# Thirty-two experts in thirteen rounds instead of sixteen, sorted by token count, with weights read in 8 KB runs

## The chip, the cores and the metric

One core of a Trainium2 chip runs the whole program. The metric is the device time of one execution in microseconds, as the median of several runs. A profiled execution gives the trace, and its own time stands beside it.

## What is computed

One layer over 512 tokens of 1,024 features, in float32. First a token mixer (a gated MLP and a differential attention, summed and projected), then a hierarchical mixture of experts, each with a residual and a layer norm. The change is in the second part:

```python
def _hier_moe(x, w_group, b_group, w_expert, b_expert, w_gate, w_up, w_down):
    g_sel = jnp.argmax(g_logits, axis=-1)                 # one of 4 groups
    top_v, top_i = lax.top_k(e_logits, EXPERT_TOPK)       # 2 of its 8 experts
    top_w = jax.nn.softmax(top_v, axis=-1) * g_w
    ...
    def expert_block(args):
        tok, wgt, e = args
        xb = t[tok]
        hb = jax.nn.silu(xb @ w_gate[e]) * (xb @ w_up[e])  # 1024 -> 512
        return (hb @ w_down[e]) * wgt[:, None]             # 512 -> 1024
```

So 1,024 pairs of a token and an expert spread over 32 experts, 32 on average. Each expert has 2 MB of gate weights, 2 MB of up weights and 2 MB of down weights, 201 MB in all, and every byte is read once. For the inputs that are run, the reference's routing gives experts 0 to 5 at most 42 tokens, the largest expert 49, and of the 26 others the twelve smallest have 21 to 30.

## The kernel before

The first half of the program is the token mixer. From about 470 us on the experts run, in **rounds** of two (`NP = E // 2` = 16 rounds, experts 2p and 2p+1 in round p). A round has 128 slots, 64 for each of the two experts (`CAP`). Per round, TensorE does this in program order (function `pair`):

- `slot_info` (L1157): which token sits in which slot, and with what weight;
- `gather_mm` (L1150), in four parts: the next round's token rows are gathered by one-hot matmuls, 64 of 128 columns, from the two fp16 parts `hs` of the hidden state;
- `glu_transpose` (L1179), `down` (L1190, two halves of 512 output columns) and `combine` (L1207), which adds the round's output to `y`;
- `gate_up` (L1103) of the next round: gate and up, each over 8 steps k of 128 input features.

In `gate_up` and `down` the two experts of a round lie side by side: 64 slots are the stationary operand, so each expert's matmul uses 64 of the array's 128 columns and writes its own half of the output's partitions (`po[j * 64:(j + 1) * 64]`); the moving operand is 512 columns of weights. Each such float32 matmul is two instructions in the trace.

**Weights.** They are cut into 192 **chunks** of 1 MB, 12 to a round (0 to 3 gate, 4 to 7 up, 8 to 11 down). A chunk holds, for both experts of a round, two steps k, and is fetched by two DMAs of 512 KB on SP's queue in `chunk_load` (L694), each with runs of 2 KB (512 floats). The last round's last two chunks are read as 512-byte runs (L690). The chunks go round a ring of 21 buffers (`AHEAD`, `ring_at`): the load of chunk i + 21 follows in SP's program behind the point where TensorE has used chunk i, and SP waits in order for the buffer to come free. One buffer of the ring (`raw`, named `craw`) is lent in round 0 to `load_lgb`, the rows of a scale and an offset that DVE uses in `scale_h`; SP's load into it waits for that, and what stands behind it on SP waits too.

**Overflow.** An expert with more than 64 tokens would be finished by a loop behind a branch (`overflow`, L1213 to L1222). All engines read the largest count into a register and branch; for these inputs the loop doesn't run. The branch stands behind round 12 (`OVERFLOW_AFTER`); the counts are made in round 1 (`counts`).

The order on every engine is the program's own here (`manual_schedule`). The last two rounds are interleaved by hand in `last_pairs`, and `finish` is the closing layer norm.

Of the kernel before, what the change touches and what calls it, by code (L numbers as in the profile page):

```python
# [21 lines left out]
D = 1024  # L22
NT = 4
# [8 lines left out]
OVERFLOW_AFTER = 12  # L32
# [11 lines left out]
def hybrid_block(ctx: ExitStack, tc: tile.TileContext, x, w_in, b_in, sg_ln_g, sg_ln_b, sg_w, sg_b,  # L44
# [30 lines left out]
    RS = const.tile([128, NT, E], F32, name="RS")  # L75
    O1 = const.tile([128, NT, E], F32, name="O1")
    Wm = const.tile([128, NT, E], F32, name="Wm")
# [596 lines left out]
    NP = E // 2  # L674
    order = [(p, c) for p in range(NP - 2) for c in range(12)]
# [3 lines left out]

    def chunk_load(dst, i, kk):  # L680
        p, c = order[i]
        if c < 8:
            src = dram((w_gate, w_up)[c // 4], (2 * p * D + 256 * (c % 4) + 128 * kk) * FF,
                       [[FF, 128], [D * FF, 2], [1, FF]])
        elif p < NP - 1 or c < 10:
            src = dram(w_down, (2 * p * FF + 256 * (c % 2) + 128 * kk) * D + 512 * ((c - 8) // 2),
                       [[D, 128], [FF * D, 2], [1, 512]])
        else:
            for j in range(2):
                nc.sync.dma_start(dst[:, j].rearrange("p (k c) -> p k c", k=4),  # L690
                                  dram(w_down, (2 * p + j) * FF * D + 512 + 256 * (c - 10) + 128 * kk,
                                       [[D, 128], [128 * D, 4], [1, 128]]))
            return
        nc.sync.dma_start(dst, src)  # L694

    held = {}

    def halves(tag):
        if tag not in held:
            if tag == "raw":  # L700
                held[tag] = [big.tile([128, 2, 512], F32, name="craw", tag="raw", bufs=2) for _ in range(2)]
            elif tag == "F1":
                held[tag] = [slot(tag, F32, (128, 2, 512))]
            else:
                c = slot(tag, F32, (128, 2, 2, 512))
                held[tag] = [c[:, kk] for kk in range(2)]
# [72 lines left out]
    aux = const.tile([128, NT, E // 2, 8], F16, name="aux")  # L779
    for t in range(NT):  # L780
        G.memset(aux[:, t, :, 1], float(128 * t))
    G.iota(aux[:, :, :, 0], pattern=[[0, NT], [0, E // 2]], base=1, channel_multiplier=1,
           allow_small_or_imprecise_dtypes=True)
# [16 lines left out]
    gbc = const.tile([128, 3, 8], F32, name="gbc")  # L800

    def fold_router():
        pgb = bank("w")
        P.transpose(pgb[:, :16], gbr, ident[:16, :16])
        V.tensor_copy(gbc[:, 0], pgb[:, 0:8])
        V.tensor_scalar(gbc[:, 1], gbc[:, 0], 1.0 / HSCALE, None, op0=OP.mult)
        V.tensor_copy(gbc[:, 2], pgb[:, 8:16])
        V.tensor_tensor(wr[:, :, 36:72], wr[:, :, 0:36], gbc[:, 2, :, None].to_broadcast([128, 8, 36]), op=OP.mult)
# [157 lines left out]
    def evacuate(pg, first=False):  # L966
# [3 lines left out]
        for d in (3,4,0,5,1,6,2,7) if first else range(8):  # L970
            src = pg[d // 4][:, (d % 4) * 128:(d % 4 + 1) * 128]
            g, b = gbc[:, 0 if first else 1, d:d + 1], gbc[:, 2, d:d + 1]
# [18 lines left out]
    def gate_weights():  # L991
# [10 lines left out]
        flat = lambda v: v.rearrange("p t e -> p (t e)")  # L1002
        ax = aux.rearrange("p t q j -> p (t q) j")[:, :, 2:8].rearrange("p q (e j) -> p q e j", j=3)
        wv, rv = [flat(v).rearrange("p (q e) -> p q e", e=2) for v in (Wm, wb)]
        V.tensor_scalar(ax[:, :, :, 0], wv, WSCALE, None, op0=OP.mult)
        V.scalar_tensor_tensor(rv, wv, WSCALE, ax[:, :, :, 0], op0=OP.mult, op1=OP.subtract)
        V.tensor_copy(ax[:, :, :, 1], rv)
        V.tensor_sub(ax[:, :, :, 2], rv, ax[:, :, :, 1])
# [85 lines left out]
    def gate_up(p, xe, filler=None):  # L1094
        pg, pu = bank("acc"), bank("acc")
        for o, base in ((pg, 0), (pu, 4)):

            ks = range(8) if p or base else (3,4,5,0,1,6,2,7)
            for k in ks:
                if filler and base and k % 2:  # L1100
# [449 lines left out]
```

## Time and profile before

| | us |
|---|---|
| median of 3 runs | 975.62 (975.32 to 977.42) |
| the profiled execution | 977.95 |
| its span, first to last instruction | 976.4 |
| TensorE busy in the span | 953.7 (98%) |
| DMA queue of SP (q1): bytes, share of 16 engines | 252.37 MB, 73.9% |
| mean granted TensorE clock | 0.993 of full speed |

All times are in us from the start of the span. A matmul's end is modelled, so a TensorE that is "busy" may still be waiting on its pipe; the starts are what to go by, and the distance from one start to the next. The share of the DMA engines counts a packet from its start to its end, and packets overlap a little, so it can pass 1.00.

### The profile page before, as it was taken

How to read it: one execution, taken by the hardware profiler on the slowest of the kernel's cores; microseconds unless marked ns; L12 is line 12 of the kernel's file. 1: busy time of each engine (PE TensorE's matmuls, PEld its weight loads, DVE VectorE, ACT ScalarE, POOL GpSimd, SP SyncE). 2: the span in 40 equal slices, each digit the busy share in tenths (PEclk: the TensorE clock that was granted, in tenths of full speed). 3: DMA queues.
4: the chain of work that ended last, by engine and by line, in shares of the span. 5: the costliest groups of instructions: out<-in, count | busy, mean ns of one | idle time of the engine just before them, and what ended most of it. 6: DMA issues, size and time to landing. Idle time of an engine off the chain costs nothing. (4 is left out here: it accounts for less than half of the span.)

```text
span 976.4 us, 14138 instructions
## 1 busy us (share of the span) xinstructions
PE 953.7 (98%) x5427; PEld 615.7 (63%) x5428; DVE 451.0 (46%) x940; ACT 300.3 (31%) x550; POOL 56.1 (6%) x97
## 2 busy tenths in 40 slices
PE   8999999999999999999999999999999999979996
PEld 6989898886888888888544444444444444434434
DVE  4567676767943423545764322333223333223236
ACT  3456565666641332323411101111101111011213
POOL 5010010110010200200000000000000000000002
PEclk9999999999999999999999999999999999989999
DMA  8634445343233758765899999999999999999972
GB/s 217 171 94 135 120 119 135 97 131 87 66 96 88 262 190 282 250 225 202 308 341 377 386 386 386 387 386 386 386 387 386 386 387 386 386 386 386 386 234 87
DMA packets 147993, 256.14 MB, mean 262 GB/s; under 512 B 11481, under 2 KB 33041, under 8 KB 147921
## 3 DMA queue, kind: packets, MB, share of 16 engines
q1 hardware_dynamic: 146672, 252.37, 73.9%
q0 software_dynamic: 1248, 2.82, 1.4%
q8 instruction: 45, 0.74, 0.3%
q14 instruction: 28, 0.22, 0.1%
HBM read 244.66 MB, written 2.10 MB: 253 GB/s over the span
## 5 line engine op out<-in xcount | busy, mean ns | idle before, releaser
L113 DVE TENSOR_TENSOR sW<-wraw,sW 128x1024 fp32r<-128x1024 f32 (+1 forms) x38 | 46.5, 1225 | 97.3 <-ACT sW L112 97.2
L112 ACT CAST sW<-wraw 128x1024 fp32r<-128x1024 f32 (+1 forms) x38 | 39.1, 1030 | 116.2 <-PE ps_w L138 65.8
L1210 DVE TENSOR_TENSOR h<-h,ps_w 128x512 f32<-128x512 f32 x112 | 69.3, 680 | 10.2 <-PE ps_w L1207 10.2
L136 PE MATMUL ps_acc<-sX,sW 128*128 128x512 f32 x184 | 73.4, 399 | 0.0
L138 PE MATMUL ps_acc<-sX,sW 128*128 128x512 f32 x184 | 72.2, 392 | 0.0
L137 PE MATMUL ps_acc<-sX,sW 128*128 128x512 f32 x184 | 72.0, 392 | 0.0
L1160 DVE TENSOR_REDUCE tid<-ps_w 128x1 f32<-128x2 f32 x14 | 2.2, 159 | 150.5 <-PE ps_w L1157 150.5
L1200 DVE SCALAR_TENSOR_TENSOR olo<-ps_acc,ws,ohi 128x512 fp32r<-128x512 f32 x28 | 21.0, 750 | 107.3 <-ACT ohi L1199 107.3
L1150 PEld LDWEIGHTS <-hs 128*128 128x128 f16 x960 | 55.0, 98 | 22.9 <-issue 22.7
L1150 PE MATMUL ps_acc<-oh,hs 128*128 128x128 f16 x960 | 63.3, 219 | 0.0
L1199 ACT ACTIVATE ohi<-ps_acc,ws 128x512 fp32r<-128x512 f32 x28 | 19.3, 688 | 135.4 <-PE ps_acc L1190 135.4
L1103 PE MATMUL ps_acc<-sX,xe 128*64 128x512 f32 x208 | 47.8, 600 | 0.0
L1172 ACT ACTIVATE sl<-ps_acc 128x512 f32<-128x512 f32 x16 | 9.5, 596 | 120.3 <-PE ps_acc L1103 120.3
L1103 PE MATMUL ps_acc<-sO,xe 128*64 128x512 f32 x200 | 45.4, 595 | 0.0
L1103 PE MATMUL ps_acc<-sS,xe 128*64 128x512 f32 x184 | 42.6, 594 | 0.0
L1182 ACT COPY hT<-ps_w 128x512 f32<-128x512 f32 x14 | 8.2, 587 | 110.1 <-PE ps_w L1179 110.1
L256 DVE TENSOR_TENSOR sW<-wraw,sW 128x1024 fp32r<-128x1024 f32 x31 | 38.3, 1241 | 7.9 <-ACT sW L252 7.2
L138 PEld LDWEIGHTS ps_acc<-sX,sW 128*128 128x128 f32 x184 | 34.5, 188 | 7.5
L136 PEld LDWEIGHTS ps_acc<-sX,sW 128*128 128x128 f32 x184 | 34.6, 188 | 6.2
L137 PEld LDWEIGHTS ps_acc<-sX,sW 128*128 128x128 f32 x184 | 34.6, 188 | 6.1
L366 PE MATMUL ps_acc<-sW,sX 128*128 128x256 f32 x128 | 36.5, 285 | 1.0 <-DVE sW L256 1.0
L365 PE MATMUL ps_acc<-sW,sX 128*128 128x256 f32 x128 | 36.9, 288 | 0.0
(372 smaller groups left out, 1937.1 us busy)
## 6 DMA issues: line engine op xcount, KB each, us to landing
wraw<-in_w_in_dram SPq DMA_DIRECT2D x32, 512.0 KB, 3.8
sO<-in_w_up_dram SPq DMA_DIRECT2D x30, 512.0 KB, 10.8
sX<-in_w_up_dram SPq DMA_DIRECT2D x30, 512.0 KB, 10.8
sS<-in_w_down_dram SPq DMA_DIRECT2D x26, 512.0 KB, 10.7
sS<-in_w_gate_dram SPq DMA_DIRECT2D x24, 512.0 KB, 10.8
sO<-in_w_down_dram SPq DMA_DIRECT2D x22, 512.0 KB, 10.8
sX<-in_w_gate_dram SPq DMA_DIRECT2D x22, 512.0 KB, 10.8
sS<-in_w_up_dram SPq DMA_DIRECT2D x22, 512.0 KB, 10.8
```

The source lines that it names most:

```text
L112: S.copy(hi, src)
L113: V.tensor_sub(lo, src, hi.bitcast(F32))
L136: P.matmul(o, lhsT=lh, rhs=rh, start=first, stop=False)
L137: P.matmul(o, lhsT=lh, rhs=rl, start=False, stop=False)
L138: P.matmul(o, lhsT=ll, rhs=rh, start=False, stop=last)
L256: V.tensor_sub(usplit[i][1], uraw[i], usplit[i][0].bitcast(F32))
L365: P.matmul(o, lhsT=xT[k][0][:, ts], rhs=hi[:, kk], start=st, stop=False, skip_group_check=True)
L366: P.matmul(o, lhsT=xT[k][0][:, ts], rhs=lo[:, kk], start=False, stop=False, skip_group_check=True)
L1103: P.matmul(o[j * 64:(j + 1) * 64, :], lhsT=xe[:, k, j * 64:(j + 1) * 64], rhs=chunk(p, base, j, k), start=k == ks[0], stop=k == ks[-1], sk ...
L1150: P.matmul(pg[d // 4][:, (d % 4) * 128:(d % 4 + 1) * 128], lhsT=hs[t][j][:, d * 128:(d + 1) * 128], rhs=ohf[:, t], start=d % 4 == 0 and t ...
L1200: V.scalar_tensor_tensor(ol, po, ws, oh.bitcast(F32), op0=OP.mult, op1=OP.subtract)
L1210: V.tensor_add(yn, yn, pcs[t])
```

## The change

**Sorting.** `sort_experts` and `order_experts` (new, in round 0) count the tokens of each expert, rank experts 6 to 31 by count with the smallest first, and permute the table of slots and weights into that order by a matmul with a permutation. Experts 0 to 5 keep their places (`FIXED`), so that rounds 0 to 2 can start before the order is known. The order goes to `cnti` as whole numbers, and SP reads one of them into a register for each of the 26 sorted places (`expert`, `values_load`).

**Rounds.** `PER = [2, 2, 2, 4, 4, 4] + [2] * 7`: rounds 3 to 5 hold the twelve smallest experts, four to a round with 32 slots each; the others hold two with 64. That is 13 rounds. The overflow branch now stands behind round 4, and compares counts with 32 or 64 by place.

**Runs.** From round 1 on, a gate or up chunk is 512 input rows of one expert: a contiguous 1 MB, of which each partition gets four neighbouring rows, 8 KB in one run. The step k of a matmul now takes every fourth row, and the gathered tokens and the transposes of the hidden layer take their features in the same order (`part_block`, `sl[:, f::4]`, and `split_h`, which writes `hs` in that order). A down chunk is likewise 8 KB a partition, half of the 16 KB of four rows, and holds both halves of the output columns. One DMA fetches a chunk; in the buffer `raw` it is two, with 4 KB runs. Round 0 and the down chunks of the last two rounds stay as they were, the latter one DMA for each expert.

```diff
+FIXED = 6
+PER = [2, 2, 2, 4, 4, 4] + [2] * 7
+PLACE = [sum(PER[:p]) for p in range(len(PER))]
-OVERFLOW_AFTER = 12
+OVERFLOW_AFTER = 4
...
+    def wide(i):
+        p, c = order[i]
+        return p > 0 and (c < 4 * PER[p] or p < NP - 2)
...
+    def expert(place):
+        if place < FIXED:
+            return slice(place, place + 1)
+        if place not in ids:
+            ids[place] = nc.values_load(
+                cnti[0:1, E + 1 + place:E + 2 + place], engines=[mybir.EngineType.SP], min_val=0, max_val=E - 1,
...
+        return ds(ids[place], 1)
...
     def chunk_load(dst, i, kk):
         p, c = order[i]
+        n = PER[p]
+        if wide(i):
+            e, part = expert(PLACE[p] + c % n), c // n % 2
+            src = w_down if c >= 4 * n else (w_gate, w_up)[c // (2 * n)]
...
+            if c >= 4 * n:
+                rows, at = slice(0, FF), at + 2048 * part
+            else:
+                rows = slice(512 * part, 512 * part + 512)
+            nc.sync.dma_start(dst, src[0][e, rows, :].rearrange("o (p i) f -> p (o i f)", i=4)[:, at:at + run])
+            return
...
     def gate_up(p, xe, filler=None):
         pg, pu = bank("acc"), bank("acc")
-        for o, base in ((pg, 0), (pu, 4)):
...
+        n = PER[p]
+        w = 128 // n
...
-                for j in range(2):
-                    P.matmul(o[j * 64:(j + 1) * 64, :], lhsT=xe[:, k, j * 64:(j + 1) * 64],
-                             rhs=chunk(p, base, j, k), start=k == ks[0], stop=k == ks[-1],
+                for j in range(n):
+                    P.matmul(o[j * w:(j + 1) * w, :], lhsT=xe[:, k, j * w:(j + 1) * w],
+                             rhs=chunk(p, m, j, k), start=k == ks[0], stop=k == ks[-1],
```

In the order of instructions that follows, a name such as sX_3633 is a buffer of the ring with its number, and x2 means that the row stands twice. On **SP's queue**, at the loads of the end of round 2 and the start of round 3, before:

```order
L694 DMA sX_3633<-in_w_up_dram 128x2x512 x2
L694 DMA craw<-in_w_down_dram 128x2x512 x2
L694 DMA sX_3768<-in_w_down_dram 128x2x512 x2
L694 DMA sS_3995<-in_w_gate_dram 128x2x512 x2
L694 DMA sS_3998<-in_w_gate_dram 128x2x512 x2
```

and now:

```order
L719 DMA sZ_3581<-in_w_up_dram 128x2048
L1295 TENSOR_LOAD cnti
L1295 ISA x2
L719 DMA sZ_3618<-in_w_up_dram 128x2048
L719 DMA sX_3650<-in_w_up_dram 128x2048
L719 DMA craw<-in_w_down_dram 128x1024 x2
...
L719 DMA sX_3783<-in_w_down_dram 128x2048
L700 TENSOR_LOAD cnti
L719 ISA
L719 DMA sS_4009<-in_w_gate_dram 128x2048
```

A pair of DMAs became one, register reads stand between the loads (ISA rows set registers), and the first read of `cnti`, for the branch, comes ahead of the load into sZ_3618.

On **DVE's queue in round 0**, between the one-hot `ohT` and the sums into `y` (h), before:

```order
L1167 TENSOR_SCALAR ohT<-tok_4385,tid 128x512
L1137 SCALAR_TENSOR_TENSOR h_2711<-h_2711,craw 128x512
L1138 SCALAR_TENSOR_TENSOR h_2711<-craw,h_2711 128x512
...
L1200 SCALAR_TENSOR_TENSOR olo<-ps_acc,ws,ohi 128x512
L1210 TENSOR_TENSOR h_2711<-h_2711,ps_w 128x512
```

and now:

```order
L1247 TENSOR_SCALAR ohT<-tok_4388,tid 128x512
L1373 SCALAR_TENSOR_TENSOR keys<-ps_w,eid 64x32
L1374 TENSOR_SCALAR keys<-eid 64x6
L1377 SCALAR_TENSOR_TENSOR oscr,col<-keys,ident 32x32 x2
L1379 SCALAR_TENSOR_TENSOR oscr,col<-ps_w,ident 32x32
L1381 SCALAR_TENSOR_TENSOR oscr,col<-keys,col,ones_b 64x32
L1385 TENSOR_SCALAR perm<-eid,col 32x32 x2
L1209 SCALAR_TENSOR_TENSOR h_2710<-h_2710,craw 128x512
...
L1282 SCALAR_TENSOR_TENSOR olo<-ps_acc,ws,ohi 128x512
L1396 CAST cnti<-ps_w 1x32
L1398 TENSOR_TENSOR over<-ps_w,cap 1x32
```

Eight small operations came ahead of the eight of `scale_h`, and nine more (the last four are those that split the weights into fp16 parts) stand between `olo` and the sums.

## Rows read from the trace of the kernel before

**Rows 1.** The page's busy times of TensorE and VectorE, and its 40 slices of the span (24.4 us each): TensorE, then the DMA engines in tenths, then what they moved.

```profile
PE 953.7 (98%) x5427; PEld 615.7 (63%) x5428; DVE 451.0 (46%) x940; ACT 300.3 (31%) x550; POOL 56.1 (6%) x97
...
PE   8999999999999999999999999999999999979996
...
DMA  8634445343233758765899999999999999999972
GB/s 217 171 94 135 120 119 135 97 131 87 66 96 88 262 190 282 250 225 202 308 341 377 386 386 386 387 386 386 386 387 386 386 387 386 386 386 386 386 234 87
```

**Rows 2.** Busy times in stretches of the expert part: the stretch, its length, PE, PEld, DVE, ACT and POOL busy (with counts), the granted clock, the share of the DMA engines, and GB/s.

```profile
500.00:530.00 30.00, 29.70 (x192) 13.58 (x190) 15.11 (x31) 3.96 (x8) 0.00 (x0) 1.00 0.98 342
530.00:700.00 170.00, 168.22 (x1057) 76.60 (x1054) 52.80 (x111) 21.66 (x43) 0.00 (x0) 1.00 1.05 386
700.00:900.00 200.00, 192.25 (x1174) 88.49 (x1174) 66.19 (x135) 25.83 (x53) 0.00 (x0) 0.98 1.05 386
```

**Rows 3.** TensorE in order of time, in one undisturbed round: start, length, what, and how many instructions.

```profile
648.61 1.94 PE L1103 MATMUL ps_acc<-sZ,xe 128*64 128x512 f32 x8
650.38 1.89 PE L1103 MATMUL ps_acc<-sX,xe 128*64 128x512 f32 x8
652.09 1.89 PE L1103 MATMUL ps_acc<-craw,xe 128*64 128x512 f32 x8
...
662.50 0.25 PE L1157 MATMUL ps_w<-aux,oh 128*128 128x8 f16 x4
662.61 1.05 PE L1150 MATMUL ps_acc<-oh,hs 128*128 128x128 f16 x16
...
665.44 1.94 PE L1190 MATMUL ps_acc<-sW,hT 128*64 128x512 f32 x8
667.21 1.89 PE L1190 MATMUL ps_acc<-sS,hT 128*64 128x512 f32 x8
669.03 1.07 PE L1150 MATMUL ps_acc<-oh,hs 128*128 128x128 f16 x16
...
678.43 1.94 PE L1103 MATMUL ps_acc<-sW,xe 128*64 128x512 f32 x8
```

**Rows 4.** SP's issues in order of time (chunk 33 begins the first row, chunk 43 is the second, the last row is the last two chunks), and from the table of DMA issues the median time from issue to landing of one kind.

```profile
505.18 3.32 SPq L694 DMA_DIRECT2D sX<-in_w_down_dram  x6
...
529.13 2.03 SPq L694 DMA_DIRECT2D sE<-in_w_up_dram  x2
...
930.15 11.78 SPq L690 DMA_DIRECT2D sE<-in_w_down_dram  x8
...
sX<-in_w_up_dram SPq DMA_DIRECT2D x30, 512.0 KB, 10.8
```

**Rows 5.** The loads of x into h, whose runs are 4 KB (a row of 1,024 floats), and two stretches (columns as in rows 2) in an earlier stage: the first with 2 KB runs alone, the second while those loads are moved.

```profile
h<-in_x_dram SPq DMA_DIRECT2D x4, 512.0 KB, 10.4
...
335.00:336.00 1.00, 1.00 (x6) 0.84 (x5) 1.00 (x2) 1.00 (x1) 0.00 (x0) 1.00 1.05 389
...
338.00:341.00 3.00, 3.00 (x15) 2.49 (x14) 0.00 (x0) 0.00 (x0) 0.00 (x0) 1.00 1.03 411
```

**Rows 6.** The overflow branch on TensorE's queue (nanoseconds), TensorE around it, and the clock in the first matmuls behind it (columns as in rows 2).

```profile
L1214 PEldq COMPARE_BRANCH  x1: 6247/6247/6247, 856.5 to 856.5; - x1
...
856.12 1.08 PE L1207 MATMUL ps_w<-olo,ohT 128*128 128x512 f32 x4
...
863.17 3.68 PE L1103 MATMUL ps_acc<-sZ,xe 128*64 128x512 f32 x8 [5.97 <-PEq L1214]
...
869.02 1.90 PE L1103 MATMUL ps_acc<-craw,xe 128*64 128x512 f32 x8
...
863.17:866.60 3.43, 3.43 (x8) 1.10 (x10) 0.00 (x0) 0.00 (x0) 0.00 (x0) 0.50 1.06 387
```

**Rows 7.** Float32 matmuls with 32 stationary columns in the attention's `mean_squares`, four of them (eight instructions) into the four quarters of one output, with what follows them on TensorE.

```profile
224.82 1.06 PE L482 MATMUL ps_w<-sq,strip 128*32 128x512 f32 x8
225.82 0.50 PE L136 MATMUL ps_acc<-sW,sX 128*128 128x512 f32 x1
```

**Rows 8.** Round 0: DVE behind `ohT`, then TensorE, where the second row is the start of round 1's gate_up, and SP's wait for the lent buffer.

```profile
484.84 0.48 DVE L1167 TENSOR_SCALAR ohT<-tok,tid 128x512 fp32r<-128x512 f32 x1
485.24 0.69 DVE L1137 SCALAR_TENSOR_TENSOR h<-h,craw 128x512 f32<-128x512 f32 x1
...
490.88 0.75 DVE L1200 SCALAR_TENSOR_TENSOR olo<-ps_acc,ws,ohi 128x512 fp32r<-128x512 f32 x1 [0.25 <-ACT ohi L1199]
...
515.63 0.18 DVE L1273 CAST cnti<-ps_w 1x32 int32<-1x32 f32 x1 [0.55 <-PE ps_w L1272]
...
491.93 1.07 PE L1207 MATMUL ps_w<-olo,ohT 128*128 128x512 f32 x4
...
499.39 5.37 PE L1103 MATMUL ps_acc<-sX,xe 128*64 128x512 f32 x24
...
497.15 7.92 SPq L694 DMA_DIRECT2D craw<-in_w_down_dram  x2
```

**Rows 9.** SP's read of one number into a register, and the register operations behind it (nanoseconds).

```profile
L1213 SPq TENSOR_LOAD <-cnti x1: 494/494/494, 894.2 to 894.2; - x1
L1213 SPq FUSED_REGOPS  x1: 182/182/182, 895.3 to 895.3; - x1
```

**Rows 10.** TensorE at the start of the seventh round from the end, in the second half of the first down matmuls of the third round from the end, and at the first and the last of the matmuls that use the program's last two chunks.

```profile
737.95 1.94 PE L1103 MATMUL ps_acc<-sE,xe 128*64 128x512 f32 x8
...
884.14 1.89 PE L1190 MATMUL ps_acc<-sS,hT 128*64 128x512 f32 x8
...
951.59 1.04 PE L1407 MATMUL ps_acc<-sE,sO 128*64 128x128 f32 x16
...
958.01 1.09 PE L1407 MATMUL ps_acc<-sE,sO 128*64 128x128 f32 x16
```

More of the change, by code (lines that the diff above doesn't have):

```diff
@@ L720, in load_chunks, with chunk @@
     def load_chunks(i0, i1):
-        for i in range(i0, min(i1, 12 * (E // 2))):
+        for i in range(i0, min(i1, len(order))):
+            tag = ring_at(i) if i else "F0"
+            if i != 1 and tag != "raw" and wide(i) and i not in chunks:
+                chunks[i] = halves(tag)
+                loaded.update(((i, 0), (i, 1)))
+                chunk_load(whole[tag], i, None)
             for kk in range(2):
                 load_half(i, kk)
-    def chunk(p, r, j, k):
-        return chunks[where[p, r + k // 2]][k % 2][:, j]
+    def chunk(p, m, j, k):
+        n = PER[p]
+        if p == 0:
+            return chunks[where[p, 4 * m + k // 2 if m < 2 else 8 + 2 * (m - 2) + k // 2]][k % 2][:, j]
+        if m < 2:
+            return chunks[where[p, (2 * m + k // 4) * n + j]][k % 4 // 2][:, k % 2]
+        if p < NP - 2:
+            return chunks[where[p, (4 + k // 2) * n + j]][k % 2][:, m - 2]
+        return chunks[where[p, 4 + 2 * m + k // 2]][k % 2][:, j]
     front = [(w_in, k2 * 256, 6144, OFF_GB, 512) for k2 in range(3, 4)]
@@ L1001, in gate_weights, with weight_parts @@
         V.tensor_add(Wm, O1, wb)
[L1002 to L1008, printed above, removed]
+        weight_parts(slice(0, FIXED), wb)
+    def weight_parts(places, rest):
+        w, r = Wm[:, :, places], rest[:, :, places]
+        a, b, c = [W3[:, :, places, i] for i in range(3)]
+        V.tensor_scalar(a, w, WSCALE, None, op0=OP.mult)
+        V.scalar_tensor_tensor(r, w, WSCALE, a, op0=OP.mult, op1=OP.subtract)
+        V.tensor_copy(b, r)
+        V.tensor_sub(c, r, b)
     mvs, rstds = {}, {}
@@ new lines, in order_experts @@
+    def order_experts(rwT):
+        pq = bank("w")
+        for t in range(NT):
+            P.matmul(pq[:, 64 * t:64 * t + 64], lhsT=rwT[0:64, t * 128:(t + 1) * 128],
+                     rhs=perm.rearrange("p a e -> p (a e)"), start=t == 0, stop=True, skip_group_check=True)
+        for i in range(2):
+            P.matmul(pq[0:1, 256 + E * i:256 + E * i + E], lhsT=col[0:32, i:i + 1], rhs=perm[0:32, 0], start=False,
+                     stop=True, skip_group_check=True)
+        V.tensor_copy(cnti[:, E + 1:], pq[0:1, 256:256 + E])
+        over = mw.tile([128, E], F32, name="over", tag="oscr")
+        V.tensor_tensor(over[0:1], pq[0:1, 256 + E:256 + 2 * E], cap[0:1], op=OP.is_gt)
+        V.tensor_copy(cnti[:, :E], over[0:1])
+        V.tensor_reduce(cnti[:, E:E + 1], over[0:1], axis=AX, op=OP.max)
+        V.tensor_copy(RW.rearrange("p t a e -> p (t a) e")[:, :, FIXED:],
+                      pq[:, 0:256].rearrange("p (q e) -> p q e", e=E)[:, :, FIXED:])
+        weight_parts(slice(FIXED, E), O1)
@@ L1336, in last_pairs @@
         l2 = ln2_params()
-        spare = [ring_at(12 * NP + i) for i in range(1, 5)]
+        spare = [ring_at(len(order) + i) for i in range(1, 5)]
         for tag in spare:
```

194 lines of the change are left out of this document (126 added, 68 removed).

## The prediction

> **What bounds the kernel now.** I began with the page's busy times and its slices [rows 1]. TensorE is busy 98% of the span, and from the 21st slice on the DMA engines are full as well, at a steady 386 GB/s. So two things stand near the limit in the expert part, and the question is which one each of them would leave behind if it got faster. The table by stretches says the same with TensorE's side in it: from 530 to 900 us TensorE and the DMA engines are both full [rows 2].
>
> A round takes TensorE from one gate_up to the next, 648.61 to 678.43: **29.82 us** [rows 3]. Its weights are 12 chunks of 1.0486 MB, and at 386 GB/s a chunk takes 2.7165 us, so a round takes the DMA engines **32.6 us**. TensorE is the faster one. It isn't seen to wait because it starts with a ring of 21 loaded chunks and eats into that lead by 2.8 us a round. How little of the lead is left at the end: chunk 43 is issued at 529.13 and lands 10.8 us later, at 539.9 [rows 4]; chunk 191 is 148 chunks behind it, so it lands at about 942 plus a few us for its short runs, and TensorE uses the last two chunks from 951.59 to 959 [rows 10]. So before, TensorE sets the end, and the DMA stream is only some 5 to 10 us behind as the next limit. **Taking work off TensorE alone is worth those few microseconds; the rest has to come from the rate of the stream.**
>
> **Part 1, three rounds fewer.** Each round has work that doesn't depend on the number of experts: a round's 29.82 us less gate_up (648.61 to 662.50, 13.89) and the two down halves (665.44 to 669.03, 3.59 each) is 8.75 us of gather, transposes and combine [rows 3]. A round of four doubles the number of expert matmuls, but each has 32 stationary columns instead of 64. Rows 7 show that form in this kernel: four such float32 matmuls, eight instructions of 512 columns, take from 224.82 to 225.82, 1.0 us together, where eight instructions with 64 columns take 1.77 (648.61 to 650.38) [rows 3, 7]. So four quarters do run side by side, and I cost a round of four at 29.8 us too. TensorE's own work falls by three rounds, 89 us. Almost none of that is on the path: it becomes waiting for weights.
>
> **Part 2, the runs.** The trace has no run of 8 KB on SP's queue. It has 2 KB (386 in the long stretch [rows 2], 389 in a short one) and 4 KB, x into h: 411 GB/s [rows 5]. Per packet, on 16 engines: 2,048 x 16 / 386 = 84.9 ns, and 4,096 x 16 / 411 = 159.5 ns. So 2 KB more cost 74.6 ns and every packet costs 10.3 ns by itself. On that line an 8 KB packet takes 159.5 + 2 x 74.6 = 308.7 ns: 425 GB/s, 2.470 us a chunk. The bounds are 2.470 (the line holds) and 2.551 (no better than the 4 KB row), and below those lies the case that nothing improves (a rival). I take **2.50 us** (419 GB/s), near the line, as two rows carry it, and a little above it for the chunks in `raw` and the 2 KB ones at the end.
>
> **Part 3, what is added.** *Sorting in round 0.* On DVE eight small operations come ahead of `scale_h`, at some 0.18 us each (a small operation on the counts took that [rows 8]), and they must wait for count matmuls that stand behind the transposes on TensorE, a microsecond or less. Behind them on DVE stands `olo`, before which DVE had just 0.25 us to spare [rows 8], so the delay passes on: matmuls with `olo` from 491.93 to about 494.3, and so everything behind, the lent buffer included, for whose load SP waits from 497.15 to 505.1 and with it chunks 33 on. Sum: **2.4 us** on the start of the steady stream and on TensorE. The bounds are 0 (the waits that follow absorb it) and 5 (the permuted reads of `split_h` also slow ACT and DVE ahead of the first gather; no row shows such reads). The nine operations of `order_experts` lie in the wait for the second down half. *Registers.* 26 reads at 0.494 us and a register operation of 0.182 per load [rows 9] on SP. SP issues once per 2.5 us with 10.8 us of loads under way [rows 4], so I cost them at nothing; without that cover, four reads at the head of a round of four are 2 us, 6 in all. The first read of `cnti` waits for the sort, but SP stands at the lent buffer soon after in any case. *The branch* costs TensorE 5.97 us of idling and, since the granted clock is 0.50 behind it, its next 16 matmul instructions 5.85 us instead of 3.48: together 8.3 us [rows 3, 6]. Behind round 4 it falls in a stretch where TensorE waits for weights: nothing on the path. *slot_info* has eight small matmuls for four: 0.11 us a round [rows 3]. *Wide down chunks* make the first down half need all chunks of its round; that is in the second sum below.
>
> **The sum.** In the profiled run chunk 33 lands at 539.9 - 10 x 2.7165 = 512.8; now at 515.2. Rounds 0 to 5 have 36 + 72 = 108 chunks. TensorE passes rounds 4 and 5 at the pace of the stream, so the last chunk of round 5 decides: 515.2 + 74 x 2.50 = 700.2. Behind it come the end of that round, 0.2 + 9.40 (669.03 to 678.43 [rows 3]), and, since TensorE has idled and may be at the lower clock, 2.4 as behind the branch: gate_up of round 6 begins at 712.2. The seven last rounds took 976.4 - 737.95 = 238.4 [rows 10], less the branch's 8.3, plus 0.8 for slot_info: 230.9. **End 943.1.** The other path: the last chunk of round 10 lands at 515.2 + 134 x 2.50 = 850.2, and from the second half of that round's first down to the end it is 976.4 - 884.14 = 92.3 [rows 10]: 942.5. The two nearly tie, so a slower stream shows in full. (The last chunk of all lands near 913, and its tail of 18.4 us behind 958.01 isn't late.) The span is then 943.1; the profiled execution was 1.55 us over its span, and 2.33 above the median of the runs: 943.1 + 1.55 - 2.33 = **942.3 us**, 3.4% less.
>
> With 2.551 us a chunk the second path gives 949.3, a time of 948.5; with 2.470 the first gives 940.9, a time of 940, and 935 if neither the sort nor the clock costs anything.
>
> **Rivals.** *The rate doesn't rise.* It is a limit of the memory or of the queue and not a cost for each packet; then the rounds saved turn wholly into waiting. Second path with 2.7165: 971.5, a time of **970.7**. For it: the rate is flat at 386 to the last digit [rows 1, 2]. Against it: 411 with longer runs in the same program [rows 5]. The Trainium skill, "DMA: Bandwidth & Descriptors", sets the least transfer for line rate at 512 B (Specifications), and says that between HBM and SBUF the HBM side, about 358 GB/s, binds (Where 436 GB/s comes from). By that rule longer runs give nothing and this rival's time holds; the trace is against both halves of it, with 386 above 358 and 411 above 386.
>
> *TensorE is slow in the rounds of four*: the quarters don't overlap in this loop as in rows 7, or the clock stays at its lower level, 1.2 of 2.4 GHz, as it did for 3.4 us behind the branch [rows 6]. With expert matmuls of twice the length a round of four takes 29.8 + 21.1 = 50.9 us. Round 3 begins at 737.95 - 6 x 29.82 + 2.4 = 561.4, and 561.4 + 3 x 50.9 + 8.3 + 230.9 = 953.3: a time of **952.5**. It costs so little because the stream needs 60 us a round of four anyway.
>
> *The other side: the stream gets slower.* The mechanism is the new addresses: the engines each step through memory 8 KB at a time, in down chunks 16 KB apart, through register-held addresses, where before all 128 partitions read neighbouring 2 KB. The change gains nothing if a chunk takes (976.4 - 515.2 - 92.3) / 134 = 2.753 us, 381 GB/s: only 1.3% below today's rate, since in the new order the last rounds have no lead left. That engines can be counted as busy and move less is in the rows: 0.98 busy at 342 GB/s from 500 to 530 [rows 2]. At that rate, 3.066 us a chunk, the end is at 1018, a time of **1017.5**. Against it: runs of 4 KB, 4 KB apart, went faster [rows 5].
>
> **How the numbers follow.** The forecast with its bounds (935 to 951) has 0.75, the slow rounds of four 0.07, the unchanged rate 0.10, a rate by chance near 381 GB/s 0.03, the slower stream 0.05. A difference of 0.2%, about 2 us, is what a measurement of this kernel can tell from none. Faster by more than that: 0.75 + 0.07 + 0.10 = 0.92; within it 0.03; slower 0.05. The range must leave out no more than 0.2: it takes in the forecast and the slow rounds of four, from 935 to 958, where the top is the second path at 400 GB/s (2.621: 958.8, a time of 958). The unchanged rate lies outside.
>
> **What would show it.** Right: 411 to 425 GB/s in the stretch from 560 to 850; gate_up of round 6 at 712, give or take 5; TensorE idle for about 53 us in rounds 4 and 5 (without waits round 6 would begin at 737.95 - 89.5 + 2.4 + 8.3 = 659), with weights' DMAs as what it waits for; a gate_up in round 3 of about 14 us. Wrong: 386 GB/s with the idle time larger; TensorE waiting for weights after round 8; a gap on SP at the reads of `cnti`; a round 1 that starts later than 499.39 + 5 = 504.4 [rows 8].

## The result and the profile after

| | before | after |
|---|---|---|
| median, us | 975.66 (975.32 to 977.42, 4 runs) | 952.61 (952.1 to 953.16, 4 runs) |
| ratio, 95% interval | | 0.976 (0.9743 to 0.9777) |
| the profiled execution, its span | 977.95, 976.4 | 953.16, 951.6 |

The kernel became 2.4% faster. The forecast was 942.3, in a range from 935 to 958: the time lies inside, but 10.3 us above the forecast.

The page of after, with TensorE, its granted clock, the DMA engines and what they moved in 40 slices of 23.8 us (before: [rows 1]):

```profile
PE   8999999999999999999989999776779999999997
...
PEclk9999999999999999999999999998889999999999
DMA  8535343533143377865587999999999999999972
GB/s 223 144 108 154 91 137 96 137 105 104 63 118 89 121 277 253 295 247 200 192 322 291 417 419 419 419 419 419 418 418 419 420 417 421 418 420 419 389 236 89
```

Where 386 stood, 419 stands, and TensorE now has a dip in slices 26 to 30. In the same columns as [rows 2], stretches of after:

```profile
500.00:530.00 30.00, 29.07 (x186) 13.26 (x186) 15.69 (x35) 3.95 (x8) 0.00 (x0) 1.00 0.82 321
560.00:850.00 290.00, 256.96 (x1702) 107.28 (x1701) 77.03 (x161) 30.34 (x62) 0.00 (x0) 0.95 1.01 419
599.00:660.00 61.00, 45.82 (x282) 15.16 (x276) 9.18 (x21) 3.95 (x8) 0.00 (x0) 0.89 1.01 419
660.00:721.00 61.00, 44.95 (x294) 15.95 (x294) 11.67 (x27) 3.95 (x8) 0.00 (x0) 0.89 1.01 418
```

The stream runs at 419 GB/s with the DMA engines full, as forecast. The last two rows are rounds 4 and 5, where TensorE idles 31 of 122 us. The first row was not forecast: from 500 to 530 the DMA engines are 0.82 busy and move 321 GB/s, where before had 0.98 and 342. TensorE in order of time shows what the idle time waits for (the start of round 3 and of its `slot_info`, the first matmul behind the overflow branch, three waits of round 5, the last weights of round 5, the start of round 6):

```profile
568.44 0.62 PE L1170 MATMUL ps_acc<-sS,xe 128*32 128x512 f32 x2
...
582.32 0.18 PE L1233 MATMUL ps_w<-tno,oh 128*128 128x2 f16 x1
...
666.60 1.03 PE L1170 MATMUL ps_acc<-sW,xe 128*32 128x512 f32 x1 [5.83 <-DMA sZ<-in_w_up_dram]
...
682.75 1.05 PE L1170 MATMUL ps_acc<-sX,xe 128*32 128x512 f32 x2 [1.46 <-DMA sX<-in_w_up_dram]
685.25 1.04 PE L1170 MATMUL ps_acc<-sX,xe 128*32 128x512 f32 x2 [1.45 <-DMA sX<-in_w_up_dram]
687.73 0.62 PE L1170 MATMUL ps_acc<-sS,xe 128*32 128x512 f32 x1 [1.44 <-DMA sS<-in_w_up_dram]
...
707.61 1.06 PE L1272 MATMUL ps_acc<-sE,hT 128*32 128x512 f32 x1 [0.58 <-DMA sE<-in_w_down_dram]
...
720.05 0.64 PE L1170 MATMUL ps_acc<-sE,xe 128*64 128x512 f32 x1
```

A gate_up with four experts takes 582.32 - 568.44 = 13.88 us, as one with two did. In round 5 TensorE advances by one chunk each 2.5 us, and waits 1.45 us of it. The last chunk of round 5 is used at 707.61 (forecast 700.2) and gate_up of round 6 starts at 720.05 (forecast 712.2). From there to the end it is 231.55 us (forecast 230.9), in which TensorE waits for no weights. So the 8 us were lost before, and they were there when round 1 began. Round 0 on TensorE, first before (gate_up of round 0, then three of the four parts of the gather; gate_up of round 1 is in [rows 8]):

```profile
469.54 1.08 PE L1103 MATMUL ps_acc<-craw,xe 128*64 128x512 f32 x4
...
483.54 1.05 PE L1150 MATMUL ps_acc<-oh,hs 128*128 128x128 f16 x16
...
485.47 1.06 PE L1150 MATMUL ps_acc<-oh,hs 128*128 128x128 f16 x16
...
490.04 1.07 PE L1150 MATMUL ps_acc<-oh,hs 128*128 128x128 f16 x16
```

and now after (the first row is gate_up of round 0, the last that of round 1):

```profile
471.31 1.08 PE L1170 MATMUL ps_acc<-craw,xe 128*64 128x512 f32 x4
...
488.30 1.86 PE L1224 MATMUL ps_acc<-oh,hs 128*128 128x128 f16 x16 [2.75 <-DVE oh L1216]
...
491.82 1.06 PE L1224 MATMUL ps_acc<-oh,hs 128*128 128x128 f16 x16
...
497.63 1.07 PE L1224 MATMUL ps_acc<-oh,hs 128*128 128x128 f16 x16
...
500.64 0.47 PE L1289 MATMUL ps_w<-ohi,ohT 128*128 128x512 f32 x1 [1.20 <-DVE RW L1401]
500.95 1.09 PE L1289 MATMUL ps_w<-olo,ohT 128*128 128x512 f32 x4
...
508.45 4.08 PE L1170 MATMUL ps_acc<-sX,xe 128*64 128x512 f32 x17
```

Before, the two gate_ups were 29.85 us apart (469.54 to 499.39), now 37.14. Set against the same places of before, 7.25 of the 7.29 us came in four steps: the first gather 2.99 later behind a one-hot that DVE made late, up to the second gather 1.59 more (the first gather took 1.86 instead of 1.05, at a granted clock of 0.50 behind the wait, and the counts and transposes of the sort stand there), 1.24 for the matmuls of `order_experts`, 1.43 for a wait of `combine` until DVE had copied the sorted table out of a PSUM bank. What ACT and DVE did ahead of the one-hot, first before:

```profile
475.82 3.90 ACT L1130 ACTIVATE hs<-h 128x1024 f16<-128x1024 f32 x4 [2.50 <-PE ps_acc L1103]
...
476.91 4.63 DVE L1131 SCALAR_TENSOR_TENSOR hs<-h,hs 128x1024 f16<-128x1024 f32 x4 [1.01 <-ACT hs L1130]
```

and now after:

```profile
477.58 8.07 ACT L1202 ACTIVATE hs<-h 128x1024 f16<-128x1024 f32 x4 [2.51 <-PE ps_acc L1170]
...
479.69 7.96 DVE L1203 SCALAR_TENSOR_TENSOR hs<-h,hs 128x1024 f16<-128x1024 f32 x4 [2.62 <-DMA sE<-in_w_down_dram]
487.56 0.68 DVE L1216 TENSOR_TENSOR oh<-io,RW 128x512 f16<-128x512 f32 x1
```

`split_h` takes 2.0 us a tile on both engines; it took 0.98 and 1.16 before. And SP's queue at the lent buffer, in after:

```profile
506.17 7.91 SPq L719 DMA_DIRECT2D craw<-in_w_down_dram  x2
514.18 1.72 SPq L719 DMA_DIRECT2D sX<-in_w_down_dram  x3
```

The loads behind it begin at 514.18; before, at 505.18 [rows 4]. That is 9.0 us, where the prediction had 2.4. They follow gate_up of round 1 as closely as before (5.73 us behind it, before 5.79), so the 9.0 us are round 0's: it began 1.77 us later and was 7.29 us longer.

### The profile page after: what moved, and what is told of

It reads as the page before. It is cut to its first block, busy times and chain, and to the rows that moved or that the text cites. A ratio compares the mean times of both kernels' runs of the same rounds, so it can differ in the third digit from the quotient of the medians.

```text
span 951.6 us, 13677 instructions
## 1 busy us (share of the span) xinstructions
PE 901.0 (95%) x5231; PEld 583.1 (61%) x5232; DVE 428.1 (45%) x904; ACT 292.8 (31%) x527; POOL 58.0 (6%) x114
## 4 chain that ended last, share of the span: by engine, by line
PE 75%; DMA 15%; DVE 7%; ACT 1%; issue 1%; SPq 0%; DVEq 0%; ACTq 0%
PE ps_acc L1170 14%; PE ps_acc L142 7%; PE ps_acc L143 7%; PE ps_acc L144 7%; PE ps_acc L1272 7%; PE ps_w L142 4%; PE ps_w L143 4%; PE ps_w L144 4%; PE ps_w L1289 4%; PE ps_acc L1224 3%; DMA sE<-in_w_down_dram 3%; DMA sO<-in_w_gate_dram 2%; DMA sZ<-in_w_up_dram 2%; DMA sW<-in_w_gate_dram 2%; DMA sS<-in_w_up_dram 2%; DMA sX<-in_w_down_dram 2%
## 5 line engine op out<-in xcount | busy, mean ns | idle before, releaser
L1170 PE MATMUL ps_acc<-sX,xe 128*64 128x512 f32 (+1 forms) x176 | 58.2, 616 | 7.2 <-DMA sX<-in_w_up_dram 7.2
L1170 PE MATMUL ps_acc<-sO,xe 128*64 128x512 f32 (+1 forms) x240 | 62.0, 603 | 2.9 <-DMA sO<-in_w_gate_dram 1.5
L1292 DVE TENSOR_TENSOR h<-h,ps_w 128x512 f32<-128x512 f32 x88 | 54.4, 679 | 7.9 <-PE ps_w L1289 7.9
L1170 PE MATMUL ps_acc<-sE,xe 128*64 128x512 f32 (+1 forms) x168 | 50.7, 683 | 1.4 <-DMA sE<-in_w_gate_dram 1.4
L1170 PE MATMUL ps_acc<-sS,xe 128*64 128x512 f32 (+1 forms) x152 | 49.6, 594 | 1.4 <-DMA sS<-in_w_up_dram 1.4
L1170 PE MATMUL ps_acc<-sW,xe 128*64 128x512 f32 (+1 forms) x112 | 45.4, 622 | 5.8 <-DMA sZ<-in_w_up_dram 5.8
L1272 PE MATMUL ps_acc<-sS,hT 128*32 128x512 f32 (+1 forms) x112 | 42.6, 631 | 2.8 <-DMA sS<-in_w_down_dram 2.8
L1170 PE MATMUL ps_acc<-sZ,xe 128*64 128x512 f32 (+1 forms) x120 | 40.3, 609 | 1.5 <-DMA sZ<-in_w_up_dram 1.5
L1272 PE MATMUL ps_acc<-sW,hT 128*32 128x512 f32 (+1 forms) x80 | 35.1, 646 | 5.1 <-DMA sW<-in_w_down_dram 5.1
L144 PEld LDWEIGHTS ps_acc<-sX,sW 128*128 128x128 f32 x184 | 34.5, 188 | 7.4
```

Source lines behind the costliest of these rows:

```text
L144: P.matmul(o, lhsT=ll, rhs=rh, start=False, stop=last)
L1170: P.matmul(o[j * w:(j + 1) * w, :], lhsT=xe[:, k, j * w:(j + 1) * w], rhs=chunk(p, m, j, k), start=k == ks[0], stop=k == ks[-1], skip_grou ...
L1272: P.matmul(po[j * w:(j + 1) * w, :], lhsT=hT[:, k, j * w:(j + 1) * w], rhs=chunk(p, 2 + n, j, k), start=k == 0, stop=k == 3, skip_group_ch ...
L1292: V.tensor_add(yn, yn, pcs[t])
```

## The experiments

Theory: these 9 us are the miss, since what is late behind the lent buffer is late to the end. Rival: a late start is swallowed where TensorE waits in rounds 4 and 5 anyway, and the 10 us lie in the stream. Every ratio is to the kernel before on the same chip.

**The two halves of the change, each alone.** First the long runs without rounds of four:

```diff
-PER = [2, 2, 2, 4, 4, 4] + [2] * 7
+PER = [2] * 16
```

> The long runs alone: sixteen rounds of two, with 8 KB runs, the sort and the rest of the change. Theory: without the rounds saved TensorE sets the end, and gains nothing from a faster stream: the time before plus round 0's delay of 9.1 us and 0.11 us a round for slot_info: 975.6 + 9.1 + 1.7 = 986 (1.011), with TensorE busy throughout and the ring full. Rival: the gain comes from the stream, and the rounds of four only go along; then the time falls to 960 or less.

986.23 us, 1.0084 (1.0069 to 1.01). Its long stretch:

```profile
560.00:850.00 290.00, 281.48 (x1762) 130.07 (x1760) 93.22 (x192) 37.64 (x77) 0.00 (x0) 0.99 1.00 410
```

TensorE is busy 281 of the 290 us (the branch's wait is 5.9 of the rest), and the stream, which did 419 in the change, is held to 410 by buffers that come free no faster: SP waits 226 of these 290 us for TensorE to free one, in the change 23. Then the rounds of four with 2 KB runs (a gate or up chunk; a down chunk is two such DMAs; features in natural order):

```diff
-                rows = slice(512 * part, 512 * part + 512)
-            nc.sync.dma_start(dst, src[0][e, rows, :].rearrange("o (p i) f -> p (o i f)", i=4)[:, at:at + run])
+                nc.sync.dma_start(dst.rearrange("p (i f) -> p i f", i=m),
+                                  src[0][e, r0:r0 + 128 * m, :].rearrange("o (i p) f -> p (o i) f", p=128))
```

> The rounds of four alone: 13 rounds as in the change, the sort too, but all weights in runs of 2 KB (a gate or up chunk in one DMA with four runs a partition, a down chunk in two DMAs for the two halves of its columns), with the features in the natural order. Theory: the stream stays at 386 GB/s, 2.7165 us a chunk, and sets the end: chunk 107 of the changed kernel was used at 707.6, so chunk 33 landed at about 522.4; 3.8 less for the plain split is 518.6, and 518.6 + 134 x 2.7165 + 92.3 = 974.9, a time of 976 (1.000), with all that the rounds save turned into waits for weights. Rival: TensorE's three rounds are worth something by themselves, 960 or less.

975.69 us, 0.9985 (0.9975 to 0.9996), within what the prediction called no difference:

```profile
560.00:850.00 290.00, 247.53 (x1559) 96.19 (x1558) 65.28 (x141) 26.30 (x54) 0.00 (x0) 0.93 1.05 386
```

TensorE idles 42 of 290 us and the stream stays at 386, though a gate chunk is one DMA of 1 MB here too. Each half alone gains nothing or next to nothing; together they gain 23 us. Both runs also carry the sort, and the first the permuted `split_h`, so round 0 is 6.1 us longer in the first and 3.6 in the second; without that the rounds of four alone would be worth some 5 us (an estimate: 1.5 + 3.6), where the prediction had 5 to 10 for work taken off TensorE alone. The same, with `split_h` in natural order too, with 4 KB runs:

```diff
+                s3 = src[0][e, r0:r0 + 256 * m, :].rearrange("o (b p i) f -> p (o b) (i f)", b=m, i=2)
```

> Rounds of four, sort and plain split as before, but runs of 4 KB: a gate or up chunk in one DMA with two runs of two rows a partition, a down chunk with two rows of 1,024 floats, features in the matching order. If each packet costs about 10 ns by itself (2 KB at 386, 4 KB at 411, 8 KB at 419 GB/s), the long stretch shows 411, 2.551 us a chunk, and the time is that of the plain split plus 134 x (2.551 - 2.5025) = 6.5 us: 956.1 (0.9775 of before). Rival: the gain is in the one DMA per chunk and not in the run's length; then 419 and 949.6 (0.971).

955.86 us, 0.978 (0.9764 to 0.9796), and in the same stretch:

```profile
560.00:850.00 290.00, 252.97 (x1664) 102.87 (x1663) 73.97 (x156) 30.16 (x62) 0.00 (x0) 0.95 1.03 409
```

409 where 411 was expected, and the time is the one expected (956.1); the rival (one DMA for each chunk is what counts) falls, here and in the run before. So the length of the run sets the rate: 386, 409 and 419 GB/s are 84.9, 160.2 and 312.8 ns for a packet of 2, 4 and 8 KB on each of 16 engines, 75.3 ns for the first 2 KB more and 76.3 for each of the next two.

**Round 0's delay, taken apart.** The permutation moved from `split_h` to the stationary operand of the gather:

```diff
-        return v[:, d % 4 * 256 + d // 4 * 128:d % 4 * 256 + d // 4 * 128 + 128]
+        return v[:, d // 4 * 512 + d % 4:d // 4 * 512 + 512:4]
...
-        S.activation(ha, hp, AF.Copy, scale=HSCALE)
+        S.activation(hs[t][0], h[t], AF.Copy, scale=HSCALE)
```

> The changed kernel, but the fp16 parts hs are written in the natural order (split_h reads h without a stride) and the permutation is made where the gather reads its stationary operand (every fourth column). Theory: the 10 us by which the forecast fell short are round 0's delay, which goes through the lent buffer to the whole stream of weights and so to the end, one to one. In the changed kernel the one-hot for round 1 came 2.99 us late behind split_h on DVE (TensorE waited 2.75), and the first gather behind the wait took 0.81 longer. Without this gate_up of round 1 should start at about 504.6 instead of 508.45, and the time be 952.6 - 3.8 = 948.8 (ratio 0.9725). Rival: round 0's delay is swallowed by the waits for weights in rounds 4 and 5 (some 28 us of TensorE), and the missing 10 us lie in the stream itself; then round 1 starts earlier but the time stays at 952.6 (0.976). Both hold only if a stationary operand with a stride costs TensorE nothing; if it does, the 16 gather matmuls that start 0.88 us ahead of the next work will take longer in every round.

949.6 us, 0.9708 (0.9694 to 0.9721). ACT, DVE and TensorE in its round 0:

```profile
474.49 3.90 ACT L1200 ACTIVATE hs<-h 128x1024 f16<-128x1024 f32 x4 [2.50 <-PE ps_acc L1170]
...
475.58 4.63 DVE L1201 SCALAR_TENSOR_TENSOR hs<-h,hs 128x1024 f16<-128x1024 f32 x4 [1.59 <-ACT hs L1200]
...
490.75 1.08 PE L1222 MATMUL ps_acc<-oh,hs 128*128 128x128 f16 x16
491.65 0.94 PE L1287 MATMUL ps_w<-ohi,ohT 128*128 128x512 f32 x3
```

`split_h` is back at 0.98 and 1.16 us a tile, the wait for the one-hot is gone, and sixteen gather matmuls still take 0.90 us to the next start (0.88 before): the stationary operand with a stride costs TensorE nothing that shows. Gate_up of round 1 stands 33.46 us behind that of round 0 (468.22 to 501.68). The time is 0.003 to 0.005 below the two measurements of the change (0.9742 and 0.976), so the rival, a delay that is swallowed later, falls. Then the sort taken out:

```diff
-            rwT = sort_experts()
...
-            order_experts(rwT)
+            weight_parts(slice(FIXED, E), O1)
```

> The changed kernel without the sort: the experts' order is 0 to 31, written once by an iota, and no largest count is found (left out: the sort, the count of what overflows, and the tokens above 32 of experts 6 to 17, which sit in the rounds of four). Theory: the sort costs about 3.4 us of round 0 (0.87 for the counts and the transposes on TensorE, 1.24 for the order's matmuls, 1.2 for the wait for its PSUM bank), gate_up of round 1 starts at about 505.0, and the time is 952.6 - 3.4 = 949.2 (0.973). Rival (round 0's delay is swallowed later): 952.6. If the first read of cnti, which stands ahead of two loads on SP, is what starves the stream and not the lent buffer, the gain is larger than the gain in the start of round 1.

948.68 us, 0.9702 (0.9683 to 0.9721); the distance is 502.08 - 469.67 = 32.41 us. SP's read of `cnti` waits for nothing here, yet the gain (3.9 us against the run just below) is no larger than what round 0 became shorter by (4.3), so nothing shows that this read starves the stream. The changed kernel once more beside these:

> The changed kernel once more, unaltered, beside the others on the same chip. 0.976 of before. What is looked for: how much the start of round 0's gate_up varies from one execution to the next (468.2 to 471.3 in the executions so far, before 469.54), and how long round 0 is from gate_up to gate_up (37.1 in the first profile, where the granted clock was 0.91 for 20 us behind the wait; 36.0 in the run with pairs alone, where it was 1.00; before 29.85).

952.74 us, 0.9742 (0.9726 to 0.9759). Here round 0 begins at 468.07, not at 471.31, and is 36.68 long: of the 9.0 us, the 1.8 by which round 0 began late differ from one execution to the next.

**What the stream does with a delay.** In the plain split, 4.34 us of DVE work more ahead of the lent buffer's release:

```diff
+            for _ in range(6):
+                V.tensor_scalar(lgb[1], lgb[1], 1.0, None, op0=OP.mult)
```

> The plain split with six operations more on DVE (a product with 1.0 over the lent buffer, 128x1024), behind scale_h's second half: the lent buffer comes free some 4 to 5 us later, and TensorE's own work isn't touched. It doubles the one wait through which the theory says that round 0's delay reaches the stream. Theory: every chunk behind the lent buffer on SP's queue is asked for that much later, nothing makes it up, and the time rises by the same 4 to 5 us, to 954 (0.976 of before). Rival: the stream is set by how fast TensorE frees buffers, and the load into the lent buffer waits beside that; then the time rises by less than half of the delay, to 951 or less.

951.91 us, 0.9745 (0.9722 to 0.9768). Its span is 950.3 (plain split: 945.8), and its round 1 starts where that of the plain split does (501.84 and 501.68). SP's queue and the stretch from 500 to 530, first in the plain split, then here:

```profile
507.39 1.72 SPq L719 DMA_DIRECT2D sX<-in_w_down_dram  x3
500.00:530.00 30.00, 29.71 (x190) 13.82 (x189) 14.86 (x29) 3.94 (x9) 0.00 (x0) 1.00 0.92 368
...
499.54 12.30 SPq L719 DMA_DIRECT2D craw<-in_w_down_dram  x2
511.94 1.32 SPq L719 DMA_DIRECT2D sX<-in_w_down_dram  x3
500.00:530.00 30.00, 29.72 (x190) 13.81 (x189) 19.03 (x35) 3.92 (x9) 0.00 (x0) 1.00 0.78 309
```

In these two executions the first load behind the lent buffer is 4.55 us later and the end 4.5 us, while TensorE began round 1 at the same time; the stream moved 59 GB/s less for 30 us, which at 419 GB/s is 4.2 us of transfer. The times of all executions say less: by the ratios it is 0.0037, 3.6 us, with intervals that leave about 1 to 6, and by the medians 2.3 us (951.91 less 949.60). So the times alone leave room for the rival (less than half); the traces are against it. `split_h` with the stride on the writing side:

```diff
-        hp = h[t].rearrange("q (m i) -> q i m", i=4)
-        ha, hb = [v.rearrange("q (i m) -> q i m", i=4) for v in hs[t]]
+        hp = h[t].rearrange("q (m i) -> q m i", i=4)
+        ha, hb = [v.rearrange("q (i m) -> q m i", i=4) for v in hs[t]]
```

> The changed kernel with split_h walking in the natural order: h is read without a stride, and the fp16 parts are written (and on DVE read again) with a stride. If it is the read of float32 with a stride of 16 bytes that costs, split_h falls back from 1.98 (ACT) and 2.0 us (DVE) for each tile to about 1.0 and 1.2; if any access with a stride costs, it stays near 2.

965.39 us, one execution. Both bounds were too low:

```profile
476.22 18.52 ACT L1202 ACTIVATE hs<-h 128x1024 f16<-128x1024 f32 x4 [2.51 <-PE ps_acc L1170]
...
481.03 18.44 DVE L1203 SCALAR_TENSOR_TENSOR hs<-h,hs 128x1024 f16<-128x1024 f32 x4 [5.32 <-ACT hs L1202]
```

4.6 us a tile. As a larger dose it fits the rest. The first load behind the lent buffer, the span, and their distance, in all executions with 8 KB runs, rounds of four and the early branch:

| kernel | load, us | span, us | distance |
|---|---|---|---|
| sort moved (below) | 506.68 | 945.2 | 438.5 |
| plain split | 507.39 | 945.8 | 438.4 |
| no sort | 507.82 | 947.2 | 439.4 |
| the change, again | 510.49 | 947.9 | 437.4 |
| lent buffer late | 511.94 | 950.3 | 438.4 |
| with GpSimd (below) | 513.20 | 952.0 | 438.8 |
| the change | 514.18 | 951.6 | 437.4 |
| stride on writing | 526.40 | 963.8 | 437.4 |

Over 20 us of delay the distance stays within 2.

**The branch** behind a round with no wait to hide it:

```diff
-OVERFLOW_AFTER = 4
+OVERFLOW_AFTER = 8
```

> The change with the overflow branch behind round 8 instead of round 4. Theory: behind round 4 the branch lies in a wait for weights and costs nothing; behind round 8 TensorE has no wait to hide it and the time rises by its 8.3 us, to 0.976 + 0.0085 = 0.9845 of before. Rival: the weights' stream sets the end everywhere, and TensorE's idling lets the ring fill and is made up for; 0.976.

959.25 us, 0.9819 (0.9798 to 0.9841): 6.5 us above the change beside it (952.74). In the profiled executions, with the first load behind the lent buffer at the same time (510.64 and 510.49), the spans are 956.7 and 947.9, 8.8 apart. The wait behind the branch, from the table of TensorE's waits (us in total, times, longest):

```profile
PE ps_acc L1170 <- PEq L1296: 5.9, 1, 5.9
```

In the change what ended that wait was a DMA of weights (the row at 666.60 above).

**Two tries at a better kernel**, both on the plain split. The first gave half of `scale_h` to GpSimd:

```diff
+                G.tensor_mul(yt, yt, lgb[1][:, 0])
+                G.tensor_add(yt, yt, lgb[1][:, 1])
```

> The plain split, and two things more in round 0. The other half of scale_h (the half that uses the lent buffer) goes to GpSimd, as a product and a sum for each of the four tiles behind one scaling on ScalarE, so that the lent buffer is free long before SP asks for it (499.4 there, 507.4 when it came free). And on DVE the sort's operations stand between the scale_h of the first two tiles and of the last two, and the copy of the sorted table stands ahead of olo, so that combine's fourth bank is free in time (1.27 us of waiting there). If the stream's start decides: round 1 starts 1.3 us earlier than with the plain split alone (32.2 us behind round 0's gate_up instead of 33.5), the load into the lent buffer doesn't wait, the rate from 500 to 530 rises from 368 towards 400, which is about 2 us of transfer, and the time is 949.6 - 1.3 - 2 = 946.3 (0.968 of before). Rival: four chunks that are asked for earlier change nothing, since TensorE frees the next buffers no earlier; then only the 1.3 us remain, 948.3 (0.970). If GpSimd's operations slow DVE's, round 1 starts later than with the plain split.

953.01 us, 0.975 (0.9736 to 0.9765), slower than the plain split. DVE, GpSimd and TensorE:

```profile
484.70 0.69 DVE L1251 SCALAR_TENSOR_TENSOR sl<-sl,ps_acc 128x512 f32<-128x512 f32 x1
...
486.25 1.77 DVE L1207 SCALAR_TENSOR_TENSOR h<-h,craw 128x512 f32<-128x512 f32 x1
...
495.75 0.69 DVE L1207 SCALAR_TENSOR_TENSOR h<-h,craw 128x512 f32<-128x512 f32 x1
...
492.57 1.59 POOL L1451 TENSOR_TENSOR h<-h,craw 128x512 f32<-128x512 f32 x1
...
495.86 1.94 PE L1392 MATMUL ps_w<-perm,rwT 64*128 64x64 f32 x8 [4.50 <-DVE perm L1386]
```

Until GpSimd's last operation ends at 494.16, `scale_h` on DVE takes 1.77 us; behind it, 0.69. TensorE waits 4.50 us for the sort. The second left GpSimd out and only moved DVE's work:

```diff
-            rwT = sort_experts()
...
-            for t in range(NT):
+            for t in range(2):
                 scale_h(V, t, 0)
+            rwT = sort_experts()
+            for t in range(2, NT):
+                scale_h(V, t, 0)
...
+        after = between() if between else None
...
+        if p == 0:
+            scale_h(V, 0, 1)
```

> The plain split, and the two DVE moves of the run with GpSimd, without GpSimd: the sort's operations between scale_h of tiles 0 and 1 and of tiles 2 and 3, the copy of the sorted table ahead of olo; and scale_h of tile 0's second half in the gap that DVE has ahead of the second olo. Theory: the wait of 1.27 us for combine's fourth bank goes, gate_up of round 1 stands 32.2 us behind that of round 0 (33.46 with the plain split alone), the lent buffer comes free some 2.6 us earlier, and the time is 949.6 - 1.3 to 949.6 - 2.6: about 947.7 (0.9694 of before). It is the control for the run with GpSimd too: there sort and scale_h came 7 us late on DVE, and if GpSimd was the reason, they keep their 0.69 us here. Rival: the order on DVE was the reason for that run's loss; then round 1 starts as late as there.

**946.73 us, 0.9677 (0.9654 to 0.97)**, the best time of the study: 3.2% less than before. Its round 0:

```profile
470.32 1.08 PE L1170 MATMUL ps_acc<-craw,xe 128*64 128x512 f32 x4
...
502.27 1.08 PE L1170 MATMUL ps_acc<-sX,xe 128*64 128x512 f32 x4
```

31.95 us from gate_up to gate_up (33.46 in the plain split): the wait for the bank is gone. The sort and the copy stood at the same places on DVE in the run with GpSimd, so its slowness came with GpSimd's work and not with that order.

## Why the prediction was right, and where it was 10 us short

**What bounds the kernel, and what the rounds and the runs are worth.** Right, and shown from both sides: rounds of four alone 0.9985, long runs alone 1.0084, both 0.976. Of the signs that the prediction named, 419 GB/s, a gate_up of 13.88 us in round 3, weights as what TensorE waits for, and no wait for weights behind round 8 came as said. Gate_up of round 6 (720.05 for 712, give or take 5) and TensorE's idle time (31 us for 53) did not, and one of its signs of being wrong was there: round 1 began at 508.45, later than 504.4.

**Part 1, a round of four at 29.8 us.** Gate_up is 13.88; the first such round takes 568.44 to 598.85, 30.4. The slow rounds of four, a rival, don't occur: the lower clock in rounds 4 and 5 (0.89 on average) falls into waits. The 53 us of idling were slack: the two rounds took 121.2 us, which less 2 x 29.8 and the branch's 8.3 is 53.3. Only 31 us show as idle time. In the rest TensorE counts as busy but is slow: two instructions of one expert by themselves take 1.05 us (at 682.75 above), where a chunk's eight take 13.88 / 16 = 0.87 side by side with those of the other experts, and a mean clock of 0.89 over 122 us can make at most 13 us of it.

**Part 2, 2.50 us a chunk.** Right: 419 GB/s are the 2.50 us that I took. The line through 2 and 4 KB alone gave 425; an 8 KB packet took 312.8 ns, where it gave 308.7. The rivals with an unchanged and with a slower stream fall with it.

**Part 3, the branch at nothing.** Right: put where nothing hides it, it cost 6.5 to 8.8 us (8.3 forecast). The registers at nothing: SP's first read of `cnti` waits 3.7 us for the sort, but the load behind it is issued at 503.95, 3.7 us after the last of the sort's counts was ready at 500.22, so its buffer came later still. Without the sort, where that read waits for nothing, the gain was no more than round 0's. The reads alone weren't taken out.

**Part 3, the sort at "2.4 us on the start of the steady stream and on TensorE".** This is the term that failed. That the lent buffer passes a delay of round 0 on to the stream was right; the size, bounded at 0 to 5, was 9.0 us in the profiled execution and 5.3 in the second one (510.49 less 505.18). Round 0 takes 36.0 us in two of four executions, 36.68 and 37.14 in the others, and 29.85 before. Four things make up the 9.0 us. First, I costed the sort on DVE alone, but its matmuls and transposes stand in TensorE's own queue, and the copy of the sorted table holds the bank that `combine` needs: 36.0 less the 32.41 without the sort is 3.6 us. Second, the permuted reads of `split_h` were a bound "0 to 5" with no row for them; the trace has that row now, twice the time, and they cost 36.0 less 33.46, 2.5 us. Third, behind TensorE's wait for the one-hot the granted clock fell to its lower level, 0.50, in two of the four executions, and round 0 was 0.7 and 1.1 us longer in these. Fourth, 1.8 us in this execution are the start of round 0, which varies by itself. The four add up to 9.0.

**The sum.** Last chunk of round 5: 7.4 us late (9.0 instead of 2.4 at the lent buffer, and 0.8 in the stretch behind). End of that round and the clock: 12.44 instead of 12.0. The last seven rounds: 0.65. From the span to the median I added 1.55 and took off 2.33 as before; now the profiled execution is only 0.55 above the median, which makes 1.8. Together 7.4 + 0.4 + 0.65 + 1.8 = 10.3. That the time still lies in the range is in part luck: the range was made wide for a slower stream and for slow rounds of four, neither of which came, and not for round 0.

The wider statement, that in a stream-bound kernel a late start is late to the end, was in the prediction only for the lent buffer, and it is what the table above shows. A delay comes to the stream through the lent buffer or through the buffers that TensorE frees, and in most runs the two move together. Two runs separate them. With the lent buffer late, TensorE's side did not move; with GpSimd, the lent buffer was free early (SP's two loads into it took 0.84 us instead of 7.9) and the next load stood 5.1 us waiting for gate_up of round 1. The distance to the end is the same in both (438.4 and 438.8). Each of these is one execution, and no run frees the lent buffer early with the rest as it was.

## What to carry to other kernels

Where two limits stand within 1%, relieve both or neither: here each half gave nothing, or 0.15%, alone. Once a stream sets the end, count what delays its steady start on every engine that its buffers pass through, TensorE's queue and PSUM banks included: in this kernel each microsecond there was a microsecond at the end. Put a permutation where a stride is free: here in the reading of a matmul's stationary operand, not in the operation that makes that operand.

## What the hardware showed that I had not expected

- A tile of 128x1024 from float32 to fp16 takes 0.98 us on ACT and 1.16 on DVE; read with a stride of 16 bytes 2.0 on both, written with a stride of 8 bytes 4.6 on both. A stationary fp16 operand with a stride of 8 bytes: nothing that shows (0.90 us against 0.88 for sixteen matmuls). The Trainium skill, "SBUF — State Buffer" (Door 1), says that accesses within one line of 16 bytes go at full rate and that each access to another line pays. The float32 reads here, each on a line of its own, agree; the fp16 writes, two to a line and 4 to 5 times as slow, don't (on DVE one of the operands is read with that stride as well).
- While GpSimd multiplies and adds 128x512 in SBUF, DVE operations with two operands in SBUF take 1.64 to 1.77 us instead of 0.69, and one with an operand in PSUM stays at 0.69. The Trainium skill, same page (Who interferes with whom), says that DVE's second SBUF input goes through a port that it shares with GpSimd, one holding it for a whole instruction; the trace agrees. It also shows something that this sentence doesn't cover: a DVE operation with one wide operand in SBUF (the one-hot `ohT`) took 1.02 us there instead of 0.48.
- A packet costs about 10 ns by itself and 75 to 76 ns for each 2 KB (84.9, 160.2 and 312.8 ns for packets of 2, 4 and 8 KB on each of 16 engines).
- The same kernel reached gate_up of round 0 at 471.31 in one execution and at 468.07 in another; the last of the program's first products starts at 17.2 and 13.9 us, so the difference was there from the beginning. What makes it isn't shown.
